# Opening of a one-core decoder layer: how the conditioning vector is broadcast, in which order the first loads are issued, and which engine makes the first operand

## The chip, the cores and the metric

The kernel runs on one core of one Trainium2 chip. The metric is device time in microseconds (us) of one launch. In the profile, PE is TensorE's matmuls, PEld its weight loads, DVE VectorE, ACT ScalarE, POOL GpSimd, and SP the engine whose queue issues most of the loads.

## The reference, cut to what matters

One decoder layer with 512 rows of 1024 features: two attention branches, gates, an output projection, a layer norm, then a gated MLP with a short convolution, and a second layer norm. A condition vector `c` of 1024 numbers sets shifts, scales and gates:

```python
mod = c @ w_ada + b_ada                      # c: (1, 1024), w_ada: (1024, 6 * 1024)
sh1, sc1, gt1, sh2, sc2, gt2 = jnp.split(mod, 6, axis=-1)
u = x * (1.0 + sc1) + sh1                    # x: (512, 1024)
proj = u @ w_in
```

So before the first column block of `u` exists, 128 numbers of the shift and 128 of the scale must be summed, each over all 1024 entries of `c`. Everything else follows from `proj`.

## The kernel before

All matrix products keep fp32 accuracy by splitting each operand into a high part (fp32r, rounded by the write) and a low part (the rest), and adding three products, high x high, low x high and high x low.

The opening works over eight feature blocks `j` of 128. For each block it loads two slices of `w_ada`, transposed beforehand so that one row holds the 1024 weights of one feature (`wa[0]` for the shift, `wa[1]` for the scale, 128 x 1024 fp32, 512 KB each), the block's rows of the projection weights (`raw`, 904 columns of seven column groups and the forget logits), and the block of `x` transposed (`xt`, 128 x 512).

`mod_sum` multiplies a `wa` slice by `cbc`, which is `c` copied to all 128 partitions, and sums along the row in the same VectorE instruction; the sum comes out by a second, short instruction that reads the accumulator. With `bcols`, the biases of `b_ada` (one is added to the scales' columns), this gives `modc`, one column of shift and one of scale. For block 0 the sums are made in halves of 512 columns, since its loads are issued in halves.

`cbc` itself is made by TensorE: `c` lies as one row in one partition (`cbr`), a column of ones times that row, in two matmuls of 512 columns (the profile shows each as two), gives the copies in two PSUM banks (`grp[0]`, `grp[1]`), and ScalarE copies these to `cbc`. Then come `WARM` matmuls on a tile of zeros, whose results nobody reads.

`first_split` makes the high part of the weights `wh` on ScalarE (for block 0 columns 0 to 384 first), `first_mod` makes the operand: `uh`, the high part of `xt * scale + shift`, the full-precision value written over `xt`, and from both the low part `ul`; `lo_of` makes low parts on VectorE. `first_pad` then makes the rest of block 0's weights (columns 384 to 904, `wh` on ScalarE and `wl` on VectorE) and a small tile of the forget logits. `first_mm` issues the matmuls of the block: five column groups with high x high, the same five with the weights' low part, the same five with the operand's low part, and later the remaining two groups and the forget logits, 23 matmuls in all, which add up in the eight PSUM banks `grp` over the eight blocks. Groups 0 to 2 use weight columns 0 to 384; groups 3 and 4 are the first that need the columns from 384 on.

SP's queue is in program order. The order on the other engines is the planner's, which follows the program and what is ready; `issue_after(i)` puts the instructions under it behind instruction `i` where they are on the same engine. No block may overtake another in the PSUM banks, and `wa` has five buffers, so the loads of later blocks wait for sums of earlier ones.

The lines of the profile that the prediction speaks of: L101 loads `cbr`, L104 `bcols`; L196 and L197 are the broadcast's matmuls and copies; L199 the `WARM` matmuls; L203 `mod_sum`; L219 to L222 block 0's loads; L244 the additions to `bcols`; L247 and L209 `modc`; L273 `uh` on ScalarE; L284 the full value of block 0 on VectorE, L279 that of later blocks on ScalarE; L90 and L93 high and low parts; L307 the matmuls of the opening.

Of the kernel before, what the change touches and what calls it, by code (L numbers as in the profile page):

```python
# [8 lines left out]
F32 = mybir.dt.float32  # L9
F32R = mybir.dt.float32r  # L10
BF16 = mybir.dt.bfloat16
AF = mybir.ActivationFunctionType
ALU = mybir.AluOpType
# [3 lines left out]
P = 128  # L17
T = 512
D = 1024
KT = D // P  # L20
# [22 lines left out]
GS = 7  # L43
SS = 10
GTILES = (3, 5, 7, 8, 12, 16, 20, 24)
WARM = 10
CUT = 5
FILL = (15, 18, 18), (11, 11, 11)


@with_exitstack
def layer_kernel(ctx: ExitStack, tc: tile.TileContext, out, xT, x, cT, crow, wa0, wa1, bcol, bgt, w1, wct, wv, bf,
                 wp, wo, lncol, lnrow, wup, cwb, wdp):
    nc = tc.nc
    ctx.enter_context(tc.manual_schedule(engines={nc.sync.engine}))
    V, S, G, PE = nc.vector, nc.scalar, nc.gpsimd, nc.tensor
# [11 lines left out]
    early = st0.enter_context(tc.tile_pool(name="early", bufs=1))  # L68
# [14 lines left out]
    def const(shape, dt, s):  # L83
        return cons.tile(shape, dt, name=s, tag=s)

    def fl(ap):
        return ap.bitcast(F32)
# [9 lines left out]
        return pre.tile(shape, dt, name=s, tag=s)  # L97

    cbc = preset([P, D], F32, "cbc")
    cbr = early.tile([1, D], F32, name="cbr", tag="cbr")  # L100
    nc.sync.dma_start(cbr, crow)  # L101
    cTs = const([P, KT], F32, "cTs")
    bcols = const([P, 4, KT], F32, "bcols")
    bcd = S.dma_start(bcols, bcol)  # L104
    warm = early.tile([P, 512], BF16, name="warm", tag="warm")
# [2 lines left out]
    ident = const([P, P], F32, "ident")  # L108
    ones = const([P, P], F32, "ones")
# [30 lines left out]
    state = {"load": 0, "proc": 0}  # L140
# [48 lines left out]
    grp = [bank() for _ in range(8)]  # L189
    pend = {}  # L190

    fpad = early.tile([P, KT, P], F32R, name="fpad", tag="fpad")
    G.memset(fl(fpad), 0.0)
    for e in range(2):
        c = slice(e * 512, (e + 1) * 512)
        PE.matmul(grp[e], ones[0:1, :], cbr[:, c], start=True, stop=True)  # L196
        S.activation(cbc[:, c], grp[e], AF.Copy)  # L197
    for n in range(WARM):
        PE.matmul(grp[5], warm[:, 0:P], warm, start=True, stop=True)  # L199

    def mod_sum(w, col, wt, c, e):
        o = modr[:, w, col, e : e + 1]
        state["read"] = V.scalar_tensor_tensor(wt[:, c], wt[:, c], 1.0, cbc[:, c], ALU.mult, ALU.mult, accum_out=o)  # L203
        return state["read"]

    def mod_col(w, col, wt):
# [4 lines left out]
    def first_load(j):  # L211
        wa = [early.tile([P, D], F32, name=nm("wa"), tag="wa", bufs=5) for _ in range(2)]
        r = stg.tile([P, 1024], F32, name=nm("raw"), tag="raw", bufs=LOADS)
        xt = z(F32, "xt")
        if j == 0:
            for e in range(2):
                c = slice(e * 512, (e + 1) * 512)
                for q in range(2):
                    nc.sync.dma_start(wa[q][:, c], wa0[j, q][:, c])  # L219
            nc.sync.dma_start(r[:, 0:384], w1[j][:, 0:384])  # L220
            nc.sync.dma_start(xt, xT[j * P : (j + 1) * P, :])
            nc.sync.dma_start(r[:, 384:W1C], w1[j][:, 384:W1C])  # L222
        else:
            nc.sync.dma_start(wa[0], wa0[j, 0])
            if j == 1:
                nc.sync.dma_start(wa[1], wa0[j, 1])
            nc.sync.dma_start(r[:, 0:W1C], w1[j])
            if j > 1:
                nc.sync.dma_start(wa[1], wa0[j, 1])
            nc.sync.dma_start(xt, xT[j * P : (j + 1) * P, :])  # L230
            if j == 6:
                nc.sync.dma_start(cTs, cT)
                nc.sync.dma_start(bfs, bf)
        pend[j] = [wa, xt, r]

    def first_acc(j):
        wa = pend[j][0]
        if j == 0:
            for e in range(2):
                for q in range(2):  # L240
                    s = mod_sum(q, j, wa[q], slice(e * 512, (e + 1) * 512), e)
            with tc.issue_after(s.ins):
                for q in (1, 3):
                    V.tensor_scalar_add(bcols[:, q, :], bcols[:, q, :], 1.0)  # L244
            for q in range(2):
                raw = modr[:, q, j, :]
                state["modc"] = V.scalar_tensor_tensor(modc[:, q, j : j + 1], raw[:, 0:1], raw[:, 1:2], bcols[:, q, j : j + 1], ALU.add, ALU.add)  # L247
        else:
            mod_col(0, j, wa[0])
            state["modc"] = mod_col(1, j, wa[1])  # L250
# [18 lines left out]
    def first_mod(j):  # L269
        wa, xt = pend[j][0:2]  # L270
        sh, sc = modc[:, 0, j : j + 1], modc[:, 1, j : j + 1]
        a, b = z(F32R, "uh"), z(F32R, "ul")
        u = state["u"] = S.activation(a, xt, AF.Identity, bias=sh, scale=sc)  # L273
        if j:
            h, l, r = pend[j][2:]
            with tc.issue_after(state["modc"].ins):
                state["after"] = lo_of(l[:, 0:W1C], r[:, 0:W1C], h[:, 0:W1C])
            with tc.issue_after(u.ins):
                u = state["u"] = S.activation(xt, xt, AF.Identity, bias=sh, scale=sc)  # L279
            with tc.issue_after(state["after"].ins):  # L280
                state["after"] = lo_of(b, xt, a)
        else:
            h, l, r = pend[j][2:]
            ts = V.tensor_scalar(xt, xt, sc, sh, ALU.mult, ALU.add)  # L284
            with tc.issue_after(ts.ins):
                ts = lo_of(l[:, 0:384], r[:, 0:384], h[:, 0:384])
            with tc.issue_after(ts.ins):
                state["after"] = lo_of(b, xt, a)
        with tc.issue_after(u.ins), tc.issue_after(state["after"].ins):
            first_pad(j)  # L290
        uh.append(a)
        ul.append(b)
# [441 lines left out]
    for p, nb in (6, 3), (7, 5):  # L734
        add_pair(p)
        for _ in range(nb):
            j = bj.pop(0)
# [255 lines left out]
    for n in range(2 * FT):  # L993
        wui.append(add_item(wup[n], split_proc))
        if n in GTILES:
            k = GTILES.index(n)
# [11 lines left out]
        if n in (28, 31, 32, 35):  # L1008
            k = (28, 31, 32, 35).index(n)
# [168 lines left out]
    r = x1  # L1178
# [126 lines left out]
def _pack(inputs):  # L1305
    import numpy as np

    a = {k: np.ascontiguousarray(v) for k, v in inputs.items()}
    c = np.ascontiguousarray
    w_in, w_ada = a["w_in"], a["w_ada"]  # L1310
    wk = w_ada.reshape(KT, P, 6, D)
    r = {}
    r["xT"] = c(a["x"][0].T)
    r["x"] = a["x"][0]
    r["cT"] = c(a["c"][0].reshape(KT, P).T)
    r["crow"] = a["c"]
    wt = c(w_ada.T).reshape(6, KT, P, D)
    r["wa0"] = c(wt[0:2].transpose(1, 0, 2, 3))
    kf = wk[:, :, [2, 5]].reshape(4, 2, P, 2, 2, 512).transpose(3, 4, 0, 2, 1, 5).reshape(2, 8, P, D)
    r["wa1"] = c(np.concatenate([kf[0], wt[3], wt[4], kf[1]], axis=0))  # L1320
    bm = a["b_ada"].reshape(6, KT, P)
    r["bcol"] = c(bm[[0, 1, 3, 4]].transpose(2, 0, 1))
    r["bgt"] = c(a["b_ada"].reshape(6, D)[[2, 5]])
    def col(kind, n):
        if kind in ("sb", "fox"):
            return (4104 if kind == "sb" else 3080) + n * P
        br, p = PAIRS[n]
        return 1544 * br + 512 * "qkv".index(kind) + p * P

    first = [w_in[:, s : s + P] for s in [col("q", 0), col("k", 0)] + [col("sb", j) for j in range(NG)]]  # L1330
    cols = np.concatenate(first + [w_in[:, 1536:1544]], axis=1)
    r["w1"] = c(cols.reshape(KT, P, W1C))
    wv = np.stack([w_in[:, 1024:1536], w_in[:, 2568:3080]])
    r["wv"] = c(wv.reshape(2, 4, 2, P, 512).transpose(0, 1, 3, 2, 4).reshape(2, 4, P, D))
    starts = [col(*t) for t in TILES]
    r["wct"] = c(np.stack([w_in[:, s : s + P].reshape(KT, P, P).transpose(1, 0, 2).reshape(P, D) for s in starts]))
    r["bf"] = c(a["b_forget"].reshape(NH, 1))
    wpj = np.stack([a["w_fox_proj"], a["w_sb_proj"]]).reshape(2, 4, P, 4, 2, P)
    r["wp"] = c(wpj.transpose(0, 3, 2, 4, 1, 5).reshape(2, 4, P, D))
    r["wo"] = c(a["w_o"].reshape(KT, P, D))  # L1340
    r["lncol"] = c(np.stack([a["ln1_g"].reshape(KT, P), a["ln1_b"].reshape(KT, P)]).transpose(2, 0, 1))
    r["lnrow"] = c(np.stack([a["ln1_g"], a["ln1_b"], a["ln2_g"], a["ln2_b"]]))
    wu = a["w_up"].reshape(KT, P, 2, FT, P)
    r["wup"] = c(wu.transpose(3, 2, 1, 0, 4).reshape(2 * FT, P, D))
    cwb = np.concatenate([a["conv_w"], a["conv_b"][None]], axis=0).reshape(4, 2, FT, P)
    r["cwb"] = c(cwb.transpose(3, 2, 1, 0).reshape(P, 2 * FT, 4))
    wd = a["w_down"].reshape(FP, 2, P, 2, 512)
    b11, b12, b21, b22 = [wd[:, m, :, n] for m in range(2) for n in range(2)]
    r["wdp"] = c(np.concatenate([b11, b12, b22, b21], axis=2))
    return r  # L1350


_NAMES = ["xT", "x", "cT", "crow", "wa0", "wa1", "bcol", "bgt", "w1", "wct", "wv", "bf", "wp", "wo", "lncol", "lnrow",
          "wup", "cwb", "wdp"]


# [17 lines left out]
```

## Time and profile before

| | us |
|---|---|
| median of three runs | 745.29 |
| lowest and highest of them | 744.9, 745.97 |
| span of the profiled execution | 743.3 |
| median less that span | 2.0 |
| first matmul of the opening's products (L307) | 9.98 |
| first matmul of block 1 | 15.58 |

The profiled execution's own device time is not recorded apart from its span; the time of a launch has about 2 us more than the span, by the median. In the rows of a timeline the first number is the start in us from the span's beginning, the second the duration of the row, then engine, line, operation and the tiles written and read; brackets hold how long the engine was idle before and what ended that. Rows of DMA issues give the size of one and the median time from issue to landing. A row of a chain gives start, duration and what the chain followed. A row of a stretch gives its bounds and length, the busy time of PE, PEld, DVE, ACT and POOL, TensorE's granted clock, and the share and rate of the DMA engines.

### The profile page before, as it was taken

What the parts mean: (1) busy time and instruction counts of PE and PEld (TensorE: products, weight loads), DVE (VectorE), ACT (ScalarE), POOL (GpSimd) and SP (SyncE); (2) the same over time, 40 slices, a digit from 0 to 9 for tenths busy, and PEclk for the clock granted to TensorE, in tenths of its full rate; (3) what the DMA queues carried; (4) which work ended last, traced back from release to release, by engine and by line L of the source; (5) the groups of instructions that cost most, each with busy time, mean ns of one, the idle gap of its engine ahead of it and who ended that gap; (6) DMA issues with size and microseconds to landing.
All of it is one profiled execution on the core that took longest, in us unless ns stands there. A gap on an engine that the chain in (4) does not pass through costs nothing.

```text
span 743.3 us, 9869 instructions
## 1 busy us (share of the span) xinstructions
PE 732.6 (99%) x3476; PEld 608.9 (82%) x3476; DVE 607.5 (82%) x1019; ACT 390.1 (52%) x683; POOL 81.5 (11%) x130
## 2 busy tenths in 40 slices
PE   8999999999999999999999999999999999999995
PEld 5878888888888888888889888888888888888885
DVE  6869789978788795884577889988887797679995
ACT  4567467586876564542055455444454444347550
POOL 1026223335010000000000000000001001000010
PEclk9999999999999999999999999999999999999998
DMA  8944454513422230642052787577788967646633
GB/s 325 405 178 134 151 197 144 171 57 116 170 77 96 101 127 29 228 173 85 1 214 86 227 287 230 196 225 235 253 299 228 253 199 212 212 156 228 230 82 85
DMA packets 45220, 131.95 MB, mean 178 GB/s; under 512 B 5905, under 2 KB 6417, under 8 KB 45170
## 3 DMA queue, kind: packets, MB, share of 16 engines
q1 hardware_dynamic: 38610, 113.66, 44.5%
q0 software_dynamic: 3536, 9.24, 6.4%
q10 hardware_dynamic: 3024, 8.41, 3.1%
q8 instruction: 27, 0.44, 0.2%
q14 instruction: 23, 0.19, 0.1%
HBM read 118.38 MB, written 12.85 MB: 177 GB/s over the span
## 4 chain that ended last, share of the span: by engine, by line
PE 98%; POOL 1%; DVE 1%; DMA 0%; issue 0%; DVEq 0%; POOLq 0%
PE ps L134 19%; PE ps L135 19%; PE ps L136 19%; PE ps L307 5%; PE ps L1103 5%; PE ps L1105 5%; PE ps L1104 5%; PE ps L559 3%; PE ps L541 2%; PE ps L458 2%; PE ps L457 2%; PE ps L459 2%; PE ps L900 2%; PE ps L901 2%; PE ps L902 2%; PE ps L483 1%
## 5 line engine op out<-in xcount | busy, mean ns | idle before, releaser
L183 ACT ACTIVATE wh<-raw 128x1024 fp32r<-128x1024 f32 (+1 forms) x105 | 109.2, 1042 | 109.5 <-PE ps L135 40.4
L93 DVE TENSOR_TENSOR wl<-raw,wh 128x1024 fp32r<-128x1024 f32 (+2 forms) x114 | 135.1, 1187 | 34.6 <-ACT wh L183 33.8
L134 PE MATMUL ps<-u2h,wh 128*128 128x512 f32 (+1 forms) x376 | 141.5, 376 | 0.0
L135 PE MATMUL ps<-u2l,wh 128*128 128x512 f32 (+1 forms) x376 | 141.2, 376 | 0.0
L136 PE MATMUL ps<-u2h,wl 128*128 128x512 f32 (+1 forms) x376 | 141.2, 376 | 0.0
L134 PEld LDWEIGHTS ps<-u2h,wh 128*128 128x128 f32 x376 | 70.8, 188 | 13.4 <-issue 0.6
L136 PEld LDWEIGHTS ps<-u2h,wl 128*128 128x128 f32 x376 | 70.8, 188 | 12.7
L135 PEld LDWEIGHTS ps<-u2l,wh 128*128 128x128 f32 x376 | 70.8, 188 | 12.6
L134 PE MATMUL ps<-uh,wh 128*128 128x512 f32 x200 | 79.5, 398 | 0.0
L135 PE MATMUL ps<-ul,wh 128*128 128x512 f32 x200 | 78.3, 391 | 0.0
L136 PE MATMUL ps<-uh,wl 128*128 128x512 f32 x200 | 78.1, 391 | 0.0
L1153 ACT ACTIVATE cv<-ps,cw 128x512 f32<-128x512 f32 x44 | 34.0, 773 | 42.4 <-PE ps L136 36.4
L1154 DVE SCALAR_TENSOR_TENSOR cv<-ps,cw,cv 128x511 f32<-128x511 f32 x44 | 32.8, 745 | 17.0 <-ACT cv L1153 17.0
L136 PEld LDWEIGHTS ps<-uh,wl 128*128 128x128 f32 x200 | 37.6, 188 | 8.2
L134 PEld LDWEIGHTS ps<-uh,wh 128*128 128x128 f32 x200 | 37.6, 188 | 7.3
L135 PEld LDWEIGHTS ps<-ul,wh 128*128 128x128 f32 x200 | 37.7, 188 | 7.1
L521 POOL TENSOR_TENSOR pt<-pt,om 128x127 f32<-128x127 f32 (+3 forms) x32 | 41.6, 1312 | 7.7 <-DVE om L520 7.7
L162 POOL DMA_DIRECT2D raw<-in_wdp x10 | 9.4, 942 | 249.2 <-DVE cv L1155 183.9
L1155 DVE SCALAR_TENSOR_TENSOR cv<-ps,cw,cv 128x510 f32<-128x510 f32 x44 | 32.7, 744 | 0.3
L1161 ACT ACTIVATE cv<-cv 128x512 f32<-128x512 f32 x22 | 13.9, 630 | 34.4 <-DVE cv L1155 34.4
L520 DVE TENSOR_TENSOR_SCAN om<-om,dg 128x127 f32<-128x127 f32 (+3 forms) x32 | 28.5, 946 | 0.1
L1105 PE MATMUL ps<-wh,hv 128*128 128x512 f32 x72 | 28.0, 389 | 0.0
(235 smaller groups left out, 1582.9 us busy)
## 6 DMA issues: line engine op xcount, KB each, us to landing
raw<-in_wup SPq DMA_DIRECT2D x44, 512.0 KB, 5.4
raw<-in_wa SPq DMA_DIRECT2D x32, 512.0 KB, 4.2
raw<-in_wct SPq DMA_DIRECT2D x25, 512.0 KB, 3.7
raw<-in_wdp SPq DMA_DIRECT2D x20, 512.0 KB, 5.4
wa<-in_wa SPq DMA_DIRECT2D x14, 512.0 KB, 8.1
raw<-in_wdp SPq DMA_DIRECT2D x22, 256.0 KB, 4.3
raw<-t SPq DMA_DIRECT2D x22, 256.0 KB, 3.8
raw<-in_wdp POOLq DMA_DIRECT2D x10, 512.0 KB, 7.7
```

The lines of the kernel that those rows point to most:

```text
L93: state["read"] = V.tensor_tensor(o, i, fl(hi), ALU.subtract)
L134: PE.matmul(ps, wh, ah, start=first, stop=False)
L135: PE.matmul(ps, wh, al, start=False, stop=False)
L136: return PE.matmul(ps, wl, ah, start=False, stop=last)
L183: state["hi"] = S.activation(h[:, 0:cols], r[:, 0:cols], AF.Copy)
L307: PE.matmul(grp[g], w, u, start=j == 0 and n == 0, stop=j == KT - 1 and n == (1 if g == 7 else 2))
L521: G.tensor_tensor(pt[b][:, s : e - 1], pt[b][:, s : e - 1], om[:, s + 1 : e], ALU.mult)
L1103: PE.matmul(ps, ah, bh, start=first, stop=False, skip_group_check=onto)
L1104: PE.matmul(ps, ah, bl, start=False, stop=False, skip_group_check=onto)
L1105: return PE.matmul(ps, al, bh, start=False, stop=last, skip_group_check=onto)
L1153: S.activation(t, ps, AF.Identity, bias=cw[:, n, 3:4], scale=cw[:, n, 2:3])
L1154: V.scalar_tensor_tensor(t[:, 1:], ps[:, 0:511], cw[:, n, 1:2], t[:, 1:], ALU.mult, ALU.add)
```

## The change

It concerns the opening alone.

- `c` is no longer loaded as a row. Its 8 columns of 128 (`cTs`, which the kernel before loaded late in the opening, by SP, for other sums) are now loaded first, by ScalarE's queue. Each column, read as 128 equal columns, is transposed by TensorE against the identity: eight fp32 transposes fill `grp[0]` and `grp[1]`.
- The sums of block 0 read the two PSUM banks; `cbc` is still copied by ScalarE for the sums of the later blocks.
- The loads of block 0 come as both halves of the shift's weights, then the scale's weights in one piece. The sums follow that order.
- The additions to `bcols` stand ahead of the sums.
- Block 0's `uh` is made by VectorE, and the full value over `xt` by ScalarE, behind it.
- `WARM` is 9 instead of 10.

```diff
-WARM = 10
+WARM = 9
...
-    cbr = early.tile([1, D], F32, name="cbr", tag="cbr")
-    nc.sync.dma_start(cbr, crow)
     cTs = const([P, KT], F32, "cTs")
+    S.dma_start(cTs, cT)
     bcols = const([P, 4, KT], F32, "bcols")
     bcd = S.dma_start(bcols, bcol)
...
+    for k in range(KT):
+        o = grp[k // 4][:, k % 4 * P : (k % 4 + 1) * P]
+        PE.transpose(o, cTs[:, k : k + 1].broadcast_to([P, P]), ident)
     for e in range(2):
-        c = slice(e * 512, (e + 1) * 512)
-        PE.matmul(grp[e], ones[0:1, :], cbr[:, c], start=True, stop=True)
-        S.activation(cbc[:, c], grp[e], AF.Copy)
+        S.activation(cbc[:, e * 512 : (e + 1) * 512], grp[e], AF.Copy)
...
-    def mod_sum(w, col, wt, c, e):
+    def mod_sum(w, col, wt, c, e, by=None):
         o = modr[:, w, col, e : e + 1]
-        state["read"] = V.scalar_tensor_tensor(wt[:, c], wt[:, c], 1.0, cbc[:, c], ALU.mult, ALU.mult, accum_out=o)
+        state["read"] = V.scalar_tensor_tensor(wt[:, c], wt[:, c], 1.0, cbc[:, c] if by is None else by, ALU.mult, ALU.mult, accum_out=o)
...
             for e in range(2):
                 c = slice(e * 512, (e + 1) * 512)
-                for q in range(2):
-                    nc.sync.dma_start(wa[q][:, c], wa0[j, q][:, c])
+                nc.sync.dma_start(wa[0][:, c], wa0[j, 0][:, c])
+            nc.sync.dma_start(wa[1], wa0[j, 1])
...
             if j == 6:
-                nc.sync.dma_start(cTs, cT)
                 nc.sync.dma_start(bfs, bf)
...
         if j == 0:
-            for e in range(2):
-                for q in range(2):
-                    s = mod_sum(q, j, wa[q], slice(e * 512, (e + 1) * 512), e)
-            with tc.issue_after(s.ins):
-                for q in (1, 3):
-                    V.tensor_scalar_add(bcols[:, q, :], bcols[:, q, :], 1.0)
+            for q in (1, 3):
+                V.tensor_scalar_add(bcols[:, q, :], bcols[:, q, :], 1.0)
+            for q in range(2):
+                for e in range(2):
+                    mod_sum(q, j, wa[q], slice(e * 512, (e + 1) * 512), e, grp[e])
...
         a, b = z(F32R, "uh"), z(F32R, "ul")
-        u = state["u"] = S.activation(a, xt, AF.Identity, bias=sh, scale=sc)
         if j:
+            u = S.activation(a, xt, AF.Identity, bias=sh, scale=sc)
...
-            ts = V.tensor_scalar(xt, xt, sc, sh, ALU.mult, ALU.add)
+            ts = V.tensor_scalar(a, xt, sc, sh, ALU.mult, ALU.add)
+            u = state["u"] = S.activation(xt, xt, AF.Identity, bias=sh, scale=sc)
```

More of the change, by code (lines that the diff above doesn't have):

```diff
@@ L51, in layer_kernel @@
 @with_exitstack
-def layer_kernel(ctx: ExitStack, tc: tile.TileContext, out, xT, x, cT, crow, wa0, wa1, bcol, bgt, w1, wct, wv, bf,
+def layer_kernel(ctx: ExitStack, tc: tile.TileContext, out, xT, x, cT, wa0, wa1, bcol, bgt, w1, wct, wv, bf,
                  wp, wo, lncol, lnrow, wup, cwb, wdp):
@@ L1315, in _pack @@
     r["cT"] = c(a["c"][0].reshape(KT, P).T)
-    r["crow"] = a["c"]
     wt = c(w_ada.T).reshape(6, KT, P, D)
@@ L1350, in _pack @@
     return r
-_NAMES = ["xT", "x", "cT", "crow", "wa0", "wa1", "bcol", "bgt", "w1", "wct", "wv", "bf", "wp", "wo", "lncol", "lnrow",
+_NAMES = ["xT", "x", "cT", "wa0", "wa1", "bcol", "bgt", "w1", "wct", "wv", "bf", "wp", "wo", "lncol", "lnrow",
           "wup", "cwb", "wdp"]
```

## The prediction, made before the changed kernel was run

> **What bounds the kernel now.** I read the page first: busy shares, slices and chain.
>
> ```profile
> span 743.3 us, 9869 instructions
> ...
> PE 732.6 (99%) x3476; PEld 608.9 (82%) x3476; DVE 607.5 (82%) x1019; ACT 390.1 (52%) x683; POOL 81.5 (11%) x130
> ...
> PE 98%; POOL 1%; DVE 1%; DMA 0%; issue 0%; DVEq 0%; POOLq 0%
> ```
>
> TensorE is busy for 99% of the span and holds 98% of the chain that ended last. A change that takes no matmul out of the body can therefore only move the moment at which the useful matmuls begin to run without gaps; behind that moment everything shifts with it. So I took the chain of waits for the first 40 us.
>
> ```profile
> 0.74 1.53 DMA cbr<-in_crow
> ...
> 2.41 3.75 PE ps L196 x4
> 6.16 4.34 PE ps L199 x10
> 10.51 29.51 PE ps L307 x130
> ```
>
> The chain runs through the broadcast of c (L196) and ten warm-up matmuls (L199), but a warm-up matmul computes nothing. What the first useful matmul (L307) waits for is read from the timelines of the three engines that make its operands, and of TensorE.
>
> ```profile
> 5.12 0.69 DVE L203 SCALAR_TENSOR_TENSOR wa<-wa,cbc 128x512 f32<-128x512 f32 x1 [3.81 <-ACT cbc L197]
> ...
> 7.08 0.69 DVE L203 SCALAR_TENSOR_TENSOR wa<-wa,cbc 128x512 f32<-128x512 f32 x1 [0.64 <-DMA wa<-in_wa]
> ...
> 7.70 0.69 DVE L203 SCALAR_TENSOR_TENSOR wa<-wa,cbc 128x512 f32<-128x512 f32 x1
> 8.31 0.08 DVE L203 DVE_READ_ACCUMULATOR wa<-wa,cbc 128x1 f32 x1
> 8.31 0.24 DVE L244 TENSOR_SCALAR bcols<-bcols 128x8 f32<-128x8 f32 x2
> 8.46 0.34 DVE L247 SCALAR_TENSOR_TENSOR modc<-modr,bcols 128x1 f32<-128x1 f32 x2
> ...
> 9.79 0.55 DVE L284 TENSOR_SCALAR xt<-xt,modc 128x512 f32<-128x512 f32 x1 [0.85 <-ACT uh L273]
> ...
> 10.72 0.68 DVE L93 TENSOR_TENSOR ul<-xt,uh 128x512 fp32r<-128x512 f32 x1
> 11.32 0.69 DVE L93 TENSOR_TENSOR wl<-raw,wh 128x520 fp32r<-128x520 f32 x1
> ```
> ```profile
> 4.49 0.60 ACT L197 ACTIVATE cbc<-ps 128x512 f32<-128x512 f32 x1 [1.85 <-PE ps L196]
> ...
> 8.94 0.81 ACT L273 ACTIVATE uh<-xt,modc 128x512 fp32r<-128x512 f32 x1 [0.23 <-DVE identb L118]
> 9.66 0.62 ACT L90 ACTIVATE wh<-raw 128x520 fp32r<-128x520 f32 x1
> ```
> ```profile
> 9.98 1.68 PE L307 MATMUL ps<-uh,wh 128*128 128x512 f32 x5
> 11.49 1.30 PE L307 MATMUL ps<-uh,wl 128*128 128x512 f32 x5
> ...
> 15.35 0.39 PE L307 MATMUL ps<-ul,fpad 128*128 128x512 f32 x1
> 15.58 1.32 PE L307 MATMUL ps<-uh,wh 128*128 128x512 f32 x5
> ```
> ```profile
> 9.91 1.32 PEld L307 LDWEIGHTS ps<-uh,wh 128*128 128x128 f32 x5 [0.28 <-ACT uh L273]
> ...
> 12.06 0.30 PEld L307 LDWEIGHTS ps<-uh,wl 128*128 128x128 f32 x2 [0.15 <-DVE wl L93]
> ```
>
> The first sum waited for the broadcast, but the third waited 0.64 us for a transfer, and the fourth followed without a gap. From there: fourth sum, read of the accumulator, two adds, two columns of modc (end 8.80), uh on ScalarE (8.94 to 9.75), first weight load 9.91, first matmul 9.98. So the broadcast no longer ends last by the third sum; the loads do. Their issue times and landings (KB, us from issue to landing):
>
> ```profile
> 0.74 0.38 ACTq L104 DMA_DIRECT2D bcols<-in_bcol  x1
> ...
> 0.74 0.34 SPq L101 DMA_DIRECT2D cbr<-in_crow  x1
> ...
> 1.14 1.78 SPq L219 DMA_DIRECT2D wa<-in_wa  x4
> ...
> 3.44 0.43 SPq L221 DMA_DIRECT2D xt<-in_xT  x1
> ```
> ```profile
> wa<-in_wa SPq DMA_DIRECT2D x1, 256.0 KB, 5.0
> ```
> ```profile
> wa<-in_wa SPq DMA_DIRECT2D x1, 256.0 KB, 5.2
> ```
> ```profile
> xt<-in_xT SPq DMA_DIRECT2D x1, 256.0 KB, 5.4
> ```
>
> The two wa rows are the third and the fourth transfer, issued alone in their windows at 2.02 and 2.49: they landed at about 7.0 and 7.7, and xt at 3.44 + 5.4 = 8.85, as late as modc. So the loads and modc are level, and the broadcast is not what the first operand waits for.
>
> **The change, part by part.** All times are of the profiled execution; 745.29 (median) less its span 743.3 leaves 2.0 us around it.
>
> *The shift in the queue.* Without cbr the first wa transfer is issued at 0.74 instead of 1.14: everything behind it lands 0.40 earlier, xt at 8.45, and all four wa pieces by 7.66 - 0.40 = 7.26. Packets of 4 KB for the second operand may save a little; I take 7.2. Bounds: the third piece landed 1.4 after the second (issued about 1.56, landed 5.6 by the 4.0 us row below), the fourth only 0.7 after the third; if the extra 0.7 does not recur, 6.5; if the shift is lost in the ramp of the queue, 7.6.
>
> ```profile
> wa<-in_wa SPq DMA_DIRECT2D x2, 256.0 KB, 4.0
> ```
>
> *The broadcast.* cT goes out on ScalarE's queue at 0.74, where bcols went and landed 1.8 us later:
>
> ```profile
> bcols<-in_bcol ACTq DMA_DIRECT2D x1, 16.0 KB, 1.8
> ```
> ```profile
> 373.89 1.91 PE L923 MATMUL ps<-ident,xn 128*128 128x128 f32 x16
> ```
>
> So transposes start near 2.6. Sixteen of them took 1.91 at full clock, 0.11 apart; at the opening's half pace 0.22, eight take 1.8: the first bank is full near 3.6, the second near 4.5. Two copies of 0.60 on ScalarE still make cbc for the later sums. The two outer products (3.75 us) go. The first two wa pieces land near 4.7 and 5.2 (0.4 before 5.1, the first sum's start and so the latest for its piece, and before 5.6), after the banks are full. The faster broadcast is hidden behind the loads and worth nothing by itself; even 1.0 us later it would cost nothing, since two sums of 0.62 would end before 7.2, when the third can begin.
>
> *Reading PSUM.* A scalar_tensor_tensor with an operand in PSUM took 690 ns, as L203 did from SBUF, so sums keep their 0.62 pitch.
>
> ```profile
> L410 DVE SCALAR_TENSOR_TENSOR s<-ps,s 64x512 fp32r<-64x512 f32 x16 | 11.0, 690 | 3.8 <-ACT s L90 3.4
> ```
>
> *Order of the loads.* Now both sums of wa[1] wait for its whole 512 KB, where before only the last one waited for the last piece. Start 7.2 + 0.1, second sum 7.92, accumulator 8.53. The adds of bcols, now ahead of the sums, leave this path (0.15), so modc ends about 0.08 + 0.34 later, 8.95: later than 8.80 although everything landed earlier.
>
> *First operand by VectorE.* From modc (8.95) TENSOR_SCALAR of 0.55 gives uh at 9.55, without the hop of 0.14 and the 0.81 of ScalarE. Weight load 0.16 behind (as 9.75 to 9.91), first matmul 9.78: 0.20 earlier than 9.98.
>
> *What is late next.* ScalarE's xt now waits for that VectorE instruction (it overwrites xt): 9.55 + 0.14 = 9.69. Behind it on ScalarE, by issue_after, is wh columns 384 and up: 0.72 after (as 8.94 to 9.66), 10.41 to 11.03. The fourth and fifth matmul need these columns: weight load 11.19, matmul about 11.30. Before, the fourth began at 11.49 - 2 x 0.227 = 11.04 (pitch from 15.35 to 15.58). So the three early matmuls run into a stall and the path is 0.26 later. VectorE's ul waits for xt too: 9.69 + 0.81 + 0.1 = 10.6, against 10.72; wl 520 at 11.2 against 11.32; then the sums of the next block, and uh of block 1, 0.1 earlier. That does not help: TensorE, not uh, then ends last, 20 matmuls on: 11.30 + 4.53 = 15.83 against 15.58. Should the planner put the three matmuls with wl 0 to 384 into the stall, it is 0, limited by the 12.06 weight load that waits for wl.
>
> *Costed at nothing.* cTs leaves the SP queue late in the stage: TensorE has no gap there (29.51 us in 130 matmuls on the chain). ScalarE issues one DMA more (0.38) ahead of its table load: covered by the wait to 3.6; uncovered it costs 0.38. bcols lands 0.4 later, near 2.9; the adds and the sums queued behind them on VectorE wait for wa until 4.7 anyhow. One warm-up matmul less: 0.43 of TensorE time that nothing waits for.
>
> *Sum.* +0.25 us: 743.3 + 0.25 + 2.0 = 745.5. With wa[1] at 6.5 and xt landing at 8.45, uh starts at 8.55, 0.45 before the 9.0 above, and the sum is -0.2; with the whole queue 0.7 earlier, -0.45; with wa[1] at 7.6, +0.65. So 744.8 to 746.0 on this path.
>
> **The rivals.**
>
> *The clock falls back (slower).* Warm-up now ends too early: transposes to 4.35, nine matmuls of 0.43, end 8.2; the first operand comes at 9.78, and after three matmuls TensorE waits again to 11.30. Before there was no gap: the warm-up ended at 10.51, into useful work. The end of the trace shows what a gap does:
>
> ```profile
> 734.94 0.28 PE L1105 MATMUL ps<-wdh,hv 128*128 128x256 f32 x1
> ```
> ```profile
> 733.97:737.38 3.41, 1.25 (x11) 1.04 (x9) 3.02 (x9) 0.29 (x1) 0.00 (x0) 1.00 0.42 156
> 737.38:740.80 3.42, 0.00 (x0) 0.00 (x0) 2.47 (x7) 0.00 (x0) 0.00 (x0) 0.50 0.25 90
> ```
>
> The columns are stretch, TensorE busy, three further engines and POOL, granted clock, DMA. By 737.38, 2.2 us after the last matmul, the clock was 0.50, and a stretch of 3.41 with 1.25 of work came before it. The opening would have stretches of 3.4 us with some 1.3 of work. A matmul at half clock costs 0.43 instead of 0.227; 3.4 us of that give 8 matmuls instead of 15, up to 1.6 us; some of it falls into the stall, so I take 1.2: 745.5 + 1.2 = 746.7, to 748 if the clock rises a further stretch late. It decides from a gap of about 1 us ahead of the first operand on. Against it: before, 4.3 us of such warm-up (L199) were enough to have the clock up from the second L307 on (five in 1.68, the next five in 1.30), 3.85 us are not far below, and the gap is an estimate.
>
> The Trainium skill ("TensorE: Matmul & The Clock Gate", Part 1) has the clock lowered only after an idle window of some 3.4 us; by it a gap of 1.6 us costs nothing, and the sum stays 745.5. The trace disagrees at its end, where 2.2 us were enough. The same page (Part 4, PE-mode transpose) says that transposes do not count as work for the gate; by that the warm-up is shorter still and the loss nearer to its 1.6; no row here shows it.
>
> *The opening gets shorter (faster).* If wa lands at 6.5 with the queue behind it, or the planner fills the stall, the start moves by 0.2 to 1.0 (the latter if xt comes 0.7 earlier too and the stall goes with it): 0.7 earlier is 744.6. For it: 0.55 instead of 0.14 + 0.81. Against it: xt at 8.45 is a floor for uh, whatever modc does.
>
> **How the numbers follow.** Forecast 745.5 (744.9 to 746.0): 40%. Clock, 746.7 (746.0 to 748): 35%. Shorter, 744.6 (743.6 to 744.9): 25%. For 8 in 10 the range leaves out the ends of both rivals: 744.3 to 747.3. A difference under 0.2%, 1.5 us, is about what cannot be told from none: below 743.8 lies 5%, a fifth of the shorter case; above 746.8, over half of the clock case, 20%; between them 75%.
>
> **What would show it.** First L307 near 9.8 behind L284, uh now written on DVE, right. A gap in PE before the fourth matmul, ended by ACT's wh 128x520: right; no gap: the planner has filled it. L199 ending near 8.2, then L307 matmuls 0.43 apart beyond 11: the clock rival. Third sum waiting on wa near 7.2: the load order; near 6.5: the shorter case. Wrong altogether if TensorE shows waits later in the stage, or if the first sums wait for the copy of a bank far beyond 5.2.

## The result and the profile after

| | median, us | range, us (runs) | profiled span, us | mean clock in it |
|---|---|---|---|---|
| before, on the same chip | 745.91 | 744.9 to 746.19 (6) | 743.3 | 0.996 |
| changed | 749.85 | 746.03 to 750.54 (6) | 747.9 | 0.993 |

The changed kernel is slower: ratio 1.005, 95% interval 1.0034 to 1.0066, or 3.9 us by the medians. The prediction was 745.5 with a range of 744.3 to 747.3, so it was wrong, and on the side of its slower rival. The changed kernel's six times go from 746.03 to 750.54, and the mean clock goes with them, roughly (0.997 in the fastest, 0.991 to 0.995 in the others).

The page first. Nothing in its busy shares tells where 4 us went; they are level with those of before.

```profile
span 747.9 us, 9873 instructions
...
PE 731.6 (98%) x3479; PEld 610.8 (82%) x3479; DVE 607.2 (81%) x1019; ACT 389.4 (52%) x683; POOL 81.6 (11%) x130
...
PE 97%; DVE 1%; DMA 1%; ACT 0%; issue 0%; SPq 0%; DVEq 0%; ACTq 0%
```

The chain of waits of the first 40 us tells it at once. Each piece is its start, its duration, and what the chain followed.

```profile
2.12 5.30 DMA raw<-in_w
...
7.44 0.52 ACT wh L90
7.96 0.49 ACT cbc L197
...
8.48 0.04 DVE wa L203
...
11.99 28.11 PE ps L306 x112
```

A load of weights (`raw`), the fourth on SP's queue, now stands ahead of the sums: ScalarE makes the high part of those weights (L90), then the copies of the banks (L197), and only then do the sums begin (L203). The timelines of ScalarE, VectorE and TensorE show the same; brackets hold how long the engine was idle and what ended that.

```profile
7.44 0.52 ACT L90 ACTIVATE wh<-raw 128x384 fp32r<-128x384 f32 x1 [4.29 <-DMA raw<-in_w]
7.87 1.06 ACT L197 ACTIVATE cbc<-ps 128x512 f32<-128x512 f32 x2
```
```profile
8.48 0.69 DVE L203 SCALAR_TENSOR_TENSOR wa<-wa,ps 128x512 f32<-128x512 f32 x1 [3.47 <-ACT cbc L197]
...
10.92 0.34 DVE L245 SCALAR_TENSOR_TENSOR modc<-modr,bcols 128x1 f32<-128x1 f32 x2
11.30 0.55 DVE L282 TENSOR_SCALAR uh<-xt,modc 128x512 fp32r<-128x512 f32 x1
```
```profile
3.78 1.94 PE L195 MATMUL ps<-ident,cTs 128*128 128x128 f32 x8 [3.78 <-DMA cTs<-in_cT]
5.51 2.84 PE L199 MATMUL ps<-warm 128*128 128x512 bf16 x9
11.99 1.62 PE L306 MATMUL ps<-uh,wh 128*128 128x512 f32 x3 [3.64 <-DVE uh L282]
...
19.76 1.07 PE L306 MATMUL ps<-uh,wh 128*128 128x512 f32 x4
```

The first sum reads `wa` and a PSUM bank (`ps`), not `cbc`, and yet it waits 3.47 us for the copy into `cbc`: two engines that read one bank are kept apart, in the order in which the program was laid out. (The run with copies last, below, has it the other way round: there a copy waits for a sum.) The banks had been full since 5.72 (3.78 + 1.94). The Trainium skill ("PSUM — Partial Sum Buffer", "PSUM bank collisions raise a hardware error") says that a dependency is put between ScalarE and VectorE on one bank even where both only read; this row agrees, and gives the price in this place.

Two losses add up. The first matmul comes at 11.99 instead of 9.98, 2.01 later. And the 23 matmuls of block 0 then take 19.76 - 11.99 = 7.77 us instead of 15.58 - 9.98 = 5.60, another 2.17. For those, the clock by stretch (bounds, length, busy PE, PEld, DVE, ACT, POOL, granted clock, DMA):

```profile
6.98:10.39 3.41, 1.36 (x7) 0.39 (x4) 1.91 (x7) 1.49 (x3) 0.00 (x0) 1.00 1.03 406
10.39:13.80 3.41, 1.81 (x4) 1.50 (x5) 2.96 (x8) 1.92 (x4) 0.00 (x0) 0.50 1.03 417
13.80:17.22 3.42, 3.42 (x9) 2.65 (x8) 3.42 (x9) 0.96 (x2) 0.00 (x0) 0.50 1.04 409
17.22:20.63 3.41, 3.41 (x16) 2.82 (x15) 2.69 (x6) 1.98 (x4) 0.00 (x0) 1.00 1.03 407
```

The column reads 1.00 ahead of a trace's first rise too, so the pace of the matmuls has to be read beside it: the nine warm-up matmuls took 2.84 us, where ten took 4.34 before. The clock had risen at 6.98, during the warm-up. It fell at 10.39, after a stretch with 1.36 us of work and the first 2 us of the gap, and it came back only at 17.22, after a stretch full of work. In the kernel before, TensorE was busy without a break from 3.5 on; the clock rose at 10.35 and stayed up:

```profile
3.52:6.93 3.41, 3.41 (x7) 0.83 (x6) 1.31 (x4) 1.19 (x2) 0.35 (x2) 1.00 0.88 275
6.93:10.35 3.42, 3.42 (x10) 1.40 (x9) 2.42 (x11) 1.93 (x4) 0.00 (x0) 1.00 1.05 419
10.35:13.76 3.41, 3.41 (x17) 2.74 (x15) 3.41 (x7) 0.52 (x2) 0.00 (x0) 1.00 1.03 411
```

So block 1 starts 2.01 + 2.17 = 4.18 us late. The last matmul starts 4.07 late (739.01, before 734.94), and the span is 4.6 longer. The half microsecond between the two lies behind the last matmul, not in the opening: from its start to the end of the span the changed kernel takes 8.87 us, the kernel before 8.33. All seven traces of kernels with the change have 8.77 to 8.95 there, all four without it 8.33.

### The profile page after: what moved, and what is told of

Its sections match the earlier page's. It is cut to its first block, busy times and chain, and to the rows that moved or that the text cites. A ratio compares the mean times of both kernels' runs of the same rounds, so it can differ in the third digit from the quotient of the medians.

```text
span 747.9 us, 9873 instructions
## 1 busy us (share of the span) xinstructions
PE 731.6 (98%) x3479; PEld 610.8 (82%) x3479; DVE 607.2 (81%) x1019; ACT 389.4 (52%) x683; POOL 81.6 (11%) x130
## 4 chain that ended last, share of the span: by engine, by line
PE 97%; DVE 1%; DMA 1%; ACT 0%; issue 0%; SPq 0%; DVEq 0%; ACTq 0%
PE ps L133 19%; PE ps L134 19%; PE ps L135 19%; PE ps L306 6%; PE ps L1102 5%; PE ps L1104 5%; PE ps L1103 4%; PE ps L558 3%; PE ps L540 2%; PE ps L457 2%; PE ps L456 2%; PE ps L458 2%; PE ps L899 2%; PE ps L900 2%; PE ps L901 2%; PE ps L481 1%
```

## The experiments

The theory after this reading: the order on ScalarE's queue alone is the cause. The planner put the high part of the weights, which waits for a load that lands at 7.4, ahead of the copies; the sums wait for the copies; the gap then costs the clock as well. Rivals: the reading of PSUM by the sums costs it (the two readers, whatever the order); the clock alone costs it; the order of the loads costs it. "Before" below is the kernel before, run on the same chip in the same job.

**Copies first on ScalarE.**

```diff
-        S.activation(cbc[:, e * 512 : (e + 1) * 512], grp[e], AF.Copy)
+        state["cp"] = S.activation(cbc[:, e * 512 : (e + 1) * 512], grp[e], AF.Copy)
...
-        hi_of(h[:, 0:W1C if j else 384], r[:, 0:W1C if j else 384])
+        with tc.issue_after(state["cp"].ins):
+            hi_of(h[:, 0:W1C if j else 384], r[:, 0:W1C if j else 384])
```

> The changed kernel, with the two copies of the PSUM banks put ahead of the high part of the first weights on ScalarE. Queue theory (the first sums wait for copies that stand on ScalarE behind an instruction that waits for the weights' load): the first sum starts near 5.6 us instead of 8.48, the third and fourth wait for wa[1] to 7.0, the first useful matmul comes near 10.0 instead of 11.99, and the time falls by about 2 us, to 747 to 748.5 (the clock still costs up to 2.7 us). Rival (the sums are held by their loads or by reading PSUM): the first sum stays at 7 us or later and the time stays at 749 to 750.5.

Measured: 744.9 us (744.21 to 745.47, 11 runs), before 745.62; ratio 0.999, interval 0.9981 to 0.9999. The whole loss is gone, which is more than was expected: the clock was to cost something still, and cost nothing. The rows of ScalarE, VectorE and TensorE:

```profile
5.80 0.60 ACT L197 ACTIVATE cbc<-ps 128x512 f32<-128x512 f32 x1 [0.26 <-PE ps L195]
7.67 0.52 ACT L90 ACTIVATE wh<-raw 128x384 fp32r<-128x384 f32 x1 [1.27 <-DMA raw<-in_w]
```
```profile
5.58 0.69 DVE L203 SCALAR_TENSOR_TENSOR wa<-wa,ps 128x512 f32<-128x512 f32 x1 [0.60 <-ACT cbc L197]
...
7.19 0.69 DVE L203 SCALAR_TENSOR_TENSOR wa<-wa,ps 128x512 f32<-128x512 f32 x1 [0.92 <-DMA wa<-in_wa]
```
```profile
5.56 3.76 PE L199 MATMUL ps<-warm 128*128 128x512 bf16 x9
10.10 0.94 PE L307 MATMUL ps<-uh,wh 128*128 128x512 f32 x3 [0.78 <-DVE uh L283]
```

The high part of the weights loses 0.23 us by standing behind the copies (7.44 to 7.67), and nothing waits for it there. The first sum still waits for a copy, 0.60 us instead of 3.47; the second waits for the second operand's load, because the planner gives the sums the order first halves, then second halves. The gap ahead of the first matmul is 0.78 us, and the clock stays up through it.

**The same fault put into the kernel before.** Only the two copies are moved, behind the first high part of the weights; the outer products, the loads, ScalarE's first operand and the ten warm-up matmuls stay.

```diff
-        S.activation(cbc[:, c], grp[e], AF.Copy)
...
-        hi_of(h[:, 0:W1C if j else 384], r[:, 0:W1C if j else 384])
+        state["split"] = S.activation(h[:, 0:W1C if j else 384], r[:, 0:W1C if j else 384], AF.Copy)
...
-    first_acc(0)
     first_split(0)
+    with tc.issue_after(state["split"].ins):
+        for e in range(2):
+            S.activation(cbc[:, e * 512 : (e + 1) * 512], grp[e], AF.Copy)
+    first_acc(0)
```

> The kernel before with one edit: on ScalarE the two copies of the broadcast stand behind the high part of the first weights. Queue theory: the copies wait for the weights' load to 8.2, the first sum starts near 8.7 instead of 5.1, the first useful matmul comes near 12.4 instead of 9.98, the warm-up ends at 10.5, and the time is 747.5 to 750.5, as slow as the changed kernel. Rival (something else in the change makes it slow): 745 to 746.5.

Measured: 749.71 us (748.39 to 750.28, 6 runs), ratio 1.0054, interval 1.0042 to 1.0066: the loss of the changed kernel, from one edit of the kernel before. Its rows are those of the changed kernel within 0.3 us as far as the first matmul. Behind it the clock was at half speed for one stretch, not two, so that block 0 takes 19.22 - 12.28 = 6.94 us, for 5.60 in the kernel before and 7.77 in the changed one:

```profile
7.39 0.52 ACT L255 ACTIVATE wh<-raw 128x384 fp32r<-128x384 f32 x1 [4.75 <-DMA raw<-in_w]
7.82 1.07 ACT L313 ACTIVATE cbc<-ps 128x512 f32<-128x512 f32 x2
```
```profile
8.43 0.69 DVE L202 SCALAR_TENSOR_TENSOR wa<-wa,cbc 128x512 f32<-128x512 f32 x1 [6.20 <-ACT cbc L313]
```
```profile
12.28 2.20 PE L306 MATMUL ps<-uh,wh 128*128 128x512 f32 x5 [2.32 <-ACT uh L272]
```
```profile
12.67:16.08 3.41, 3.41 (x10) 2.67 (x9) 3.41 (x8) 1.14 (x3) 0.00 (x0) 0.50 1.02 411
```

**The sums from SBUF.** The changed kernel, with the sums of block 0 reading `cbc` instead of the banks.

```diff
-                    mod_sum(q, j, wa[q], slice(e * 512, (e + 1) * 512), e, grp[e])
+                    mod_sum(q, j, wa[q], slice(e * 512, (e + 1) * 512), e)
```

> The changed kernel, its first sums reading cbc in SBUF again. Queue theory: the sums waited for the copies anyway, so the first one starts at 8.5 us as in the changed kernel, and the time stays at 748 to 750.5. Rival (reading PSUM by VectorE is what delays the sums, by a slower read or by a conflict with the copies): the first sum starts 0.5 us or more earlier and the time falls by 1 us or more.

Measured: 748.89 us (747.5 to 750.54, 5 runs), ratio 1.0046, interval 1.0031 to 1.0061. The first sum starts at 8.67, against 8.48, and still waits for the copies. So the reading of PSUM is not the cause; in the changed kernel it had simply lost its use, since the sums waited for the copies with it or without it. Nor is it the reason for ScalarE's order: with sums that read `cbc` again, as in the kernel before, the planner still puts the copies behind the high part of the weights.

```profile
7.63 0.52 ACT L90 ACTIVATE wh<-raw 128x384 fp32r<-128x384 f32 x1 [4.46 <-DMA raw<-in_w]
8.05 1.07 ACT L197 ACTIVATE cbc<-ps 128x512 f32<-128x512 f32 x2
```
```profile
8.67 0.69 DVE L203 SCALAR_TENSOR_TENSOR wa<-wa,cbc 128x512 f32<-128x512 f32 x1 [3.51 <-ACT cbc L197]
```

**Copies last.** The changed kernel with the copies behind the sums, so that the sums read the banks first. On ScalarE the copies then stand behind the high part of the weights too.

```diff
-    for e in range(2):
-        S.activation(cbc[:, e * 512 : (e + 1) * 512], grp[e], AF.Copy)
...
+    for e in range(2):
+        S.activation(cbc[:, e * 512 : (e + 1) * 512], grp[e], AF.Copy)
```

> The changed kernel with the copies of the two banks moved behind the four first sums, so that the sums wait for TensorE and their loads alone. Queue theory: the first sum starts when the first bank is full, near 5.0 us, the second (of wa[1]) waits for its load to 7.1, the first useful matmul comes near 10.0, as with the copies first, and the time is that of the kernel with the copies first, 744.3 to 745.5. Rival (the broadcast's own speed is worth something beyond the queue): the first useful matmul comes at 9.6 or earlier and the time lies 0.4 us or more below 744.9.

Measured: 745.33 us (744.73 to 746.16, 11 runs), ratio 0.9997, interval 0.9988 to 1.0005. The first sum now starts at 4.98 without a wait, 0.60 us ahead of the run with copies first, and the second begins at 7.15 all the same, on the second operand's load. What the direct reading gains is lost again there: with the copies out of the way, the loads decide. The second copy now waits 0.51 us for a sum: the two readers of a bank are kept apart in this order too.

```profile
4.98 0.69 DVE L201 SCALAR_TENSOR_TENSOR wa<-wa,ps 128x512 f32<-128x512 f32 x1
...
7.15 0.69 DVE L201 SCALAR_TENSOR_TENSOR wa<-wa,ps 128x512 f32<-128x512 f32 x1 [1.48 <-DMA wa<-in_wa]
```
```profile
9.16 0.60 ACT L311 ACTIVATE cbc<-ps 128x512 f32<-128x512 f32 x1 [0.51 <-DVE wa L201]
```
```profile
10.05 0.93 PE L304 MATMUL ps<-uh,wh 128*128 128x512 f32 x3 [1.78 <-DVE uh L280]
```

**The clock apart from the path.** The changed kernel with `WARM = 22` instead of 9, so that the warm-up reaches into the first operand and there is no gap.

> The changed kernel with WARM at 22 instead of 9. The warm-up then lasts to 11 to 12 us, up to the first operand. Clock theory (the gap of 3.6 us before the first useful matmul lets the clock fall to half): the first useful matmul stays near 12.0, no matmul after it is 0.43 apart, the mean clock is 0.996 to 0.997, and the time is 746 to 747. Queue theory alone (the clock costs nothing): 749 to 750.5, as with 9.

Measured: 747.38 us (746.85 to 748.33, 10 runs), ratio 1.0024, interval 1.0015 to 1.0033. The clock does not fall, the first matmul is as late as in the changed kernel (12.11 for 11.99), and about half of the loss is gone: 1.005 less 1.0024 is 0.0026 of 746, or 1.9 us.

```profile
5.45 6.77 PE L199 MATMUL ps<-warm 128*128 128x512 bf16 x22
12.11 0.93 PE L306 MATMUL ps<-uh,wh 128*128 128x512 f32 x3
13.39 0.72 PE L306 MATMUL ps<-uh,wh 128*128 128x512 f32 x2 [0.35 <-ACT wh L90]
...
18.08 0.61 PE L306 MATMUL ps<-uh,wh 128*128 128x512 f32 x2
```

By these rows block 1 starts 19.76 - 18.08 = 1.7 us earlier than in the changed kernel, which agrees. Here, without other matmuls to put into it, the stall ahead of the fourth matmul shows, as the prediction had it.

**The clock alone.** The kernel before with `WARM = 4` instead of 10.

> The kernel before with WARM at 4 instead of 10: the warm-up ends near 7.8 us, the first useful matmul stays at 9.98, nothing else changes. Clock theory: a gap of 2.2 us is enough; the mean clock falls to 0.991 to 0.995 in most runs and the time is 747 to 748.5. Rival (a gap of 2.2 us is too short to lower the clock, as only an idle window of 3.4 us would): 745 to 746.2, as before.

Measured: 746.68 us (745.89 to 749.6, 11 runs), ratio 1.0019, interval 1.0008 to 1.0031. That is below what was expected, and the mean clock did not fall either (0.996 to 0.998); the column counts the time ahead of the first rise as full. The run does not show the clock fall: it had not risen at all before 15.71, so what it prices is a late rise. The first matmul comes earlier than in the kernel before (9.55 for 9.98): 0.25 us of it because its operand was begun earlier in this execution (8.69 for 8.94), the rest because six warm-up matmuls no longer stand in front of it. Block 1 comes later (17.79 against 15.58), because its predecessors run at half pace up to 15.71.

```profile
9.55 2.50 PE L307 MATMUL ps<-uh,wh 128*128 128x512 f32 x5 [1.71 <-ACT uh L273]
11.85 2.33 PE L307 MATMUL ps<-uh,wl 128*128 128x512 f32 x5
...
17.79 1.07 PE L307 MATMUL ps<-uh,wh 128*128 128x512 f32 x4
```

**First operand by VectorE alone.** The kernel before with only that part of the change.

```diff
-        u = state["u"] = S.activation(a, xt, AF.Identity, bias=sh, scale=sc)
         if j:
+            u = S.activation(a, xt, AF.Identity, bias=sh, scale=sc)
...
-            ts = V.tensor_scalar(xt, xt, sc, sh, ALU.mult, ALU.add)
+            ts = V.tensor_scalar(a, xt, sc, sh, ALU.mult, ALU.add)
+            u = state["u"] = S.activation(xt, xt, AF.Identity, bias=sh, scale=sc)
```

> The kernel before with one part of the change: the first operand by VectorE and the full value over xt by ScalarE behind it. Theory of the prediction: the first useful matmul comes 0.3 to 0.4 us earlier, near 9.6, but the fourth waits for the weights' columns from 384 on, which now stand on ScalarE behind xt, and comes near 11.1 instead of 11.04: time 745.3 to 746, no change to tell. Rival (the shorter operand carries through): the fourth matmul comes near 10.7 and the time falls by 0.3 us or more, below 745.3.

Measured: 745.38 us (744.42 to 746.18, 11 runs), ratio 0.9996, interval 0.9987 to 1.0004: no difference that can be told. The operand is ready at 9.15 (8.61 + 0.54), and the first matmul still starts at 9.98, behind the tenth warm-up matmul. The weight loads of the warm-up are 0.43 apart (9.06, 9.49), and the first of L308 follows at 9.91 in the same step. In the kernel before the times are the same (9.05, 9.48, 9.91), so the warm-up stood on its path too, level with `uh`.

Block 1 comes later here than in the kernel before, 16.18 for 15.58, since the clock rose at 11.59 and not at 10.35, though TensorE had done the same work by then. Half pace thus hides whether the fourth matmul would have waited for its weights, and this trace does not decide between theory and rival. The last row is the third sum's: here it waits for the broadcast's second copy, in the kernel before it waited for a load.

```profile
6.10 4.45 PE L199 MATMUL ps<-warm 128*128 128x512 bf16 x10
9.98 2.26 PE L308 MATMUL ps<-uh,wh 128*128 128x512 f32 x5
...
16.18 1.07 PE L308 MATMUL ps<-uh,wh 128*128 128x512 f32 x4
```
```profile
6.83 0.69 DVE L203 SCALAR_TENSOR_TENSOR wa<-wa,cbc 128x512 f32<-128x512 f32 x1 [0.39 <-ACT cbc L197]
```

**Copies first, sums in the order of the loads.** To the run with copies first this adds that the sums of the scale stand behind both of the shift.

```diff
-            for q in range(2):
+            for e in range(2):
+                first = mod_sum(0, j, wa[0], slice(e * 512, (e + 1) * 512), e, grp[e])
+            with tc.issue_after(first.ins):
                 for e in range(2):
-                    mod_sum(q, j, wa[q], slice(e * 512, (e + 1) * 512), e, grp[e])
+                    mod_sum(1, j, wa[1], slice(e * 512, (e + 1) * 512), e, grp[e])
```

> The changed kernel with the copies first, and the four first sums held in the order of their loads (both of wa[0], then both of wa[1]), which the planner had mixed. Queue theory: the sums of wa[0] run at 5.6 and 6.3, those of wa[1] at 7.2 and 7.8, modc and with it the first useful matmul come 0.6 us earlier than with the copies first alone, near 9.5, and block 1 too: 744.3. Rival (the next wait is as late: the stall for the weights' columns from 384 on, or block 1's operand): the first matmul is earlier, block 1 starts at 15.6 as with the copies first alone, and the time stays at 744.9.

**Copies first, loads in the old order.** The other way to bring sums and loads into one order: first halves, then second halves, on both.

```diff
-                nc.sync.dma_start(wa[0][:, c], wa0[j, 0][:, c])
-            nc.sync.dma_start(wa[1], wa0[j, 1])
+                for q in range(2):
+                    nc.sync.dma_start(wa[q][:, c], wa0[j, q][:, c])
```

> The changed kernel with ScalarE's two copies of the banks ahead of the high part of the weights, as before, and the loads of block 0 in the order of the kernel before (first halves of shift and scale, then second halves). It is the partner of the run with copies first and sums in the order of the loads (first matmul at 9.38). If the order of the loads costs what the prediction put on it (the second pair of sums waits for the whole of the second operand, 0.08 to 0.3 us), this order has its first sum at 4.9 to 5.5, its third near 6.9, modc by 8.3 and the first matmul at 9.2 to 9.5; time 744.0 to 744.6. Rival: the last piece lands as late as the whole second operand does (6.9), and the sums, held by copies to 5.5, end no earlier either way: first matmul within 0.2 of 9.38 and time the same. Against both: the sums are not made in the order of the loads and wait again, first matmul near 10.1, time 744.9.

Measured: 744.18 us (743.98 to 745.8, 11 runs), ratio 0.9985, interval 0.9976 to 0.9994, with sums in the order of the loads; 744.07 us (743.72 to 744.66, 11 runs), ratio 0.9983, interval 0.9974 to 0.9992, with loads in the old order. They cannot be told apart, and both beat both kernels: the kernel before by some 1.2 us (a small gain, though both intervals lie below 1), and the changed one by some 5 (1.005 less 0.9984 of 746). TensorE in the two, and the first operand of the second:

```profile
9.38 0.93 PE L309 MATMUL ps<-uh,wh 128*128 128x512 f32 x3
```
```profile
9.23 0.94 PE L307 MATMUL ps<-uh,wh 128*128 128x512 f32 x3 [0.68 <-DVE uh L283]
```
```profile
8.54 0.55 DVE L283 TENSOR_SCALAR uh<-xt,modc 128x512 fp32r<-128x512 f32 x1 [0.23 <-DMA xt<-in_xT]
```

That is 0.60 and 0.75 ahead of the kernel before, and 0.7 to 0.9 ahead of the run with copies first alone. Block 1 keeps the gain: it starts at 14.89 and 14.74, for 15.58 in the kernel before. `modc` is complete at 8.66 in the first run and at 8.31 in the second, but there `uh` then waits 0.23 us for `xt`, so that 0.15 is left of the difference. What mattered was that sums and loads have one order; which of the two, the times do not tell.

## Why the prediction was wrong, point by point

- *The broadcast* is the step that failed, in its sentence that two copies of 0.60 on ScalarE still make `cbc`. They were counted as two instructions with no place in ScalarE's order and no one waiting for them, though they read the same banks as the sums. In the kernel before, the copies came early (4.49). In the changed one the planner put the high part of the weights ahead of them, and that waits for a load until 7.42. "Even 1.0 us later it would cost nothing" fits the run with copies first, whose sums still waited for a load at 7.19; but the sums came 3.4 us later than in the kernel before (8.48 against 5.12). Why the planner changed the order stays open: it is not that the sums no longer read `cbc`, since the run with sums from SBUF has the same order. The run with copies first and the same fault in the kernel before show it from both sides. The prediction's last line named the sign to look for; the step should have named its price.
- In the same step, the transposes were to start near 2.6 and begin at 3.78: `cTs` landed 2.9 us after its issue, not the 1.8 of `bcols`, from which its landing was taken. Eight transposes took 1.94, for 1.8 predicted. This 1.2 us late start cost nothing, as the run with copies last shows: the sums waited for loads later on.
- The prediction also took from one trace that the loads, not the broadcast, end last ahead of the third sum (7.08). In the run with the first operand by VectorE, whose opening is the same up to there, that sum waited for the broadcast's second copy, to 6.83, and with `WARM = 4` to 6.69. So the two were level within some 0.3 us, and which ends last changes from execution to execution.
- *Reading PSUM*: a sum from PSUM took 0.69, as predicted, and from SBUF too.
- *The shift in the queue*: right in kind, a little too cautious. The second operand was there for the sum at 7.15 or 7.19, for 7.2 + 0.1 predicted.
- *Order of the loads*: that the scale's sums wait for its whole load is right only in the program's order; the planner interleaved them, and so the second sum waited (0.92 and 1.48 us in the two runs above). Put into the loads' order, the new order has the first matmul 0.15 us later than the old one (9.38 and 9.23), which the times cannot tell (744.18 and 744.07). That `xt` is a floor for `uh` came true in the second of these runs (8.54, for 8.45 and a hop).
- *First operand by VectorE*: the 0.55 was right. The gain was not to be had in the kernel before, where the tenth warm-up matmul ended the wait at 9.98; the prediction did not put the warm-up on that path, where the weight load of 9.91 had come in step with the warm-up's. With nine, and with the sums on time, the first matmul came at 9.23.
- *What is late next*: the stall ahead of the fourth matmul shows with 22 warm-up matmuls: TensorE is idle for 0.35 us, and the fourth starts 1.28 us behind the first (13.39 and 12.11), for 1.52 predicted (11.30 and 9.78). In the changed kernel the planner put the three matmuls with `wl` into it, as the prediction allowed.
- *The clock falls back* came true, with its mark (matmuls 0.43 apart beyond 11), and larger than priced: 2.17 us in block 0 for 1.2. That is the case in which the clock rises a further stretch late, which the prediction named. With one stretch at half speed, as in the same fault put into the kernel before and in the run with sums from SBUF, block 0 took 1.34 and 1.31 us more (6.94 and 6.91 for 5.60), near the price. Its cause was not the one given, a warm-up that ends too early under a timely operand: in the runs with copies first or last, with the same nine matmuls, the clock stayed up; with copies last the gap was 1.78 us, and the matmuls behind it ran at full pace, so it does not decide from a gap of about 1 us on, as the prediction had it. The rule of the Trainium skill ("TensorE: Matmul & The Clock Gate", Part 1) that the prediction weighed, with a drop only after an idle stretch of some 3.4 us, does not fit: the clock fell after a stretch that still held 1.36 us of work.
- *Costed at nothing*: the additions to `bcols` stand ahead of the sums, and their load landed at 4.6 in the changed kernel, not near 2.9. No sum waited for them there. With loads in the old order the first sum came right behind them (additions at 5.12, sum at 5.52), and the wait for `xt` hid it.
- *The sum* has no term for what comes behind the last matmul, which is about 0.5 us longer in every trace of a kernel with the change.

Not settled: what makes that end longer; and the changed kernel's fastest run, 746.03, whose opening was not recorded. Its mean clock, 0.997, is that of executions whose clock did not fall, but it is still faster than the late path alone would let it be by the run with 22 warm-up matmuls (746.85 at best).

## What to carry to other kernels

When a change lets a consumer read a value straight from a bank, list every reader of that bank, and ask on which queue it stands and what load the instruction ahead of it waits for. An instruction that "still does the same" is not free until its place in its engine's order is known. And where warm-up work holds a clock, price every delay of the first operand twice: once for the path, once for the clock that the gap takes away.

## What was not expected of the hardware

- Whether the clock falls goes by the work in one stretch of 3.41 us, not by the gap. In these traces it fell after stretches with 0.68 (sums from SBUF), 1.09 (the same fault put into the kernel before) and 1.36 us of work (the changed kernel), and at the kernel's end after 1.35 (`WARM = 4`). It stayed up after one with 1.64 (copies last, 6.76 to 10.18), which held the whole gap of 1.78 us, and at the end of the run with sums from SBUF after one with 1.59. So the limit lies between 1.36 and 1.59 us in these traces.

```profile
3.35:6.76 3.41, 2.90 (x11) 2.15 (x12) 1.06 (x5) 0.00 (x0) 0.00 (x0) 1.00 1.01 321
6.76:10.18 3.42, 1.64 (x8) 0.64 (x7) 2.99 (x10) 1.84 (x4) 0.00 (x0) 1.00 1.02 401
```

- To rise it needs more. It rose at 6.76 with copies last, after the 2.90 us of the first row above, and did not after 1.81 us of work in the changed kernel (10.39 to 13.80), nor after 2.75 with `WARM = 4`:

```profile
8.89:12.30 3.41, 2.75 (x7) 2.17 (x8) 2.77 (x6) 1.24 (x3) 0.00 (x0) 1.00 1.01 412
```

This stretch lies ahead of its trace's first rise, so its 1.00 says nothing; the pace does, five matmuls in 2.50 us and 2.33, against 1.32 at full clock.

- Not all busy time counts. In the kernel before the stretch from 3.52 to 6.93 was full, and yet the clock did not rise at its end: the warm-up ran at half pace, ten matmuls in 4.34 us, and the rise came at 10.35. Most of that stretch, up to 6.16, was the broadcast's outer products, whose operands have one row. Either such matmuls count for less, or they were not at work all the time that the profile, which models the ends of matmuls, counts as busy; no run separates the two.

- The stretches do not begin with the program. In three traces whose TensorE work starts within 0.03 us of each other (outer products at 2.39 to 2.42, then ten warm-up matmuls), the clock first rose at 9.26, 10.35 and 11.59: the same fault put into the kernel before, the kernel before, and the first operand by VectorE. So the time that a late rise or a fall costs should differ between executions of one kernel as well; no kernel was traced twice.

- A stretch filled by transposes and a short warm-up was enough to raise the clock at 6.98 in the changed kernel (3.57 to 6.98, of which the transposes are 1.94). The Trainium skill ("TensorE: Matmul & The Clock Gate", Part 4, PE-mode transpose) says that transposes do not count as work for the gate; these fp32 transposes did, since the warm-up alone fills only 1.5 us of that stretch, and 2.75 us of matmuls were too few with `WARM = 4`. The profile lists them as MATMUL and does not show whether they ran in that mode.
